# Modulation products brought forward by one stage in a two-layer diffusion backbone

## The chip, the cores and the metric

The kernel runs on one core of a Trainium2 chip. The metric is the device time of one execution in microseconds (us). PE is TensorE (PEld its weight loads), DVE VectorE, ACT ScalarE, POOL GpSimd, SP SyncE, whose queue issues most DMAs. A PSUM bank holds 128x512 floats; the kernel has eight.

## The reference: what is computed

Two layers work on 256 latent tokens of width 1024 beside 256 context tokens. Each layer first makes six modulation vectors of width 1024 for the latent and six for the context stream: `silu(c) @ w_mod[l] + b_mod[l]`. Vectors 0 and 1 (shift and scale) modulate the normalised input of the input projection. Vector 2 is the gate of the attention's result, 3 and 4 modulate the input of the mixture of experts, and 5 is its gate. Then come the input projection, three kinds of attention with 16 heads in all, an output projection with a residual and a layer norm, a router that picks two of 32 experts for a token, and the experts, with a second residual and norm. Only the latent stream is returned, so the second layer leaves the context tokens out after its attention.

## The kernel before, in words

One large function writes the whole program out. A scheduler then puts the instructions of each engine in a fixed order: an instruction that comes earlier in the program goes first, unless its inputs or its buffer are not there yet by the scheduler's own reckoning, in which case a later one may be put ahead.

**Weights** arrive as tiles of up to 1 MB (128 partitions of 2048 floats) in the order of one list, `stream`. `pump` (lines 146 to 164) issues loads from the head of the list while the tiles that are loaded and unused fill at most `cap[0]` units of 1 MB and a unit is free; it is called after each tile that is dropped. SP issues the loads, except those of experts whose number the router decides: these go through POOL (line 142) and can only be issued when the routing is done. The cap is 6 units at the start, `AC[0]` = 5 from the first layer's input projection on, `OC[0]` = 3 in its output projection and `MC[0]` = 11 ahead of its experts.

**Modulation** comes in three groups of two vectors for each layer, 8 tiles of 1 MB to a group. `mod_steps(l, g)` (lines 310 to 330) makes 8 steps for group 1 or 2: a step takes one tile and multiplies it by the activated conditioning, four products of 128 x 512 into the four column groups of one bank of tag "e" (line 320). The last step adds the bias and turns the result over with four transposes in `mod_cols` (line 369). `mod0_steps(l, tag)` (lines 332 to 362) does group 0 in another layout. Here a step has two halves: `one(j)` multiplies one tile (eight products of 128 x 256, line 347) and ACT copies the result out of its bank (line 351); `two(j)` turns that copy over with two transposes into a second bank (line 357), and DVE reduces it and adds the bias (lines 358 and 360). For the second layer the banks are of tag "a", of which there are four.

These steps are the **fillers**: functions in a list, which `fill(n)` takes from the front and runs at the place where it is called. For the first layer's run the list holds 24 steps: group 1 and group 2 of layer 0, then group 0 of layer 1. The first layer's own group 0 is no filler; it is made inside `lead` (lines 541 to 567), with the first columns of the input projection.

**The first layer's stages**, in order: `lead`, the rest of the input projection (`p_b`, `p_cq`, `p_qa`, `p_v`, lines 742 to 748; every product there is done as three passes over split operands, lines 455 to 457, after `split` has made the two parts on ACT and DVE, lines 449 and 450), a short stage that builds heads (lines 795 to 824), the attention, the output projection with the router, and the experts. The attention is a loop over 24 units and two empty rounds: each round issues `score(u)`, which takes two banks of tag "a" for the scores (lines 872 and 874) and hands them to DVE (line 882) and ACT (line 884) for the softmax, then `turn(u - 2)` (transposes, lines 896 and 902, and after every third unit the product with the values, lines 917 and 923), then one filler. In layer 0 a filler is taken only while more than 8 are left, so 16 are used in the attention and 8 remain.

The output projection runs over four blocks of 128 tokens with a lag of two blocks: `stage1(b)` does the products and the norm (`deepnorm`, whose last instruction is ACT at line 436), `stage2(b)` transposes the result (line 1054), modulates it (lines 1059 and 1061) and computes the router's logits (lines 1064 to 1066), `stage3(b)` transposes back (line 1073). `route` follows after every second block. The 8 steps that remain are taken there: `FA` gives 3 after `stage1(3)`, `FI` gives 2 and 4 after `stage2(2)` and `stage2(3)`. After it DVE finishes the routing (up to line 1403), PE gathers the tokens for the first experts (line 1189), and `up` (line 1202) starts the experts. The experts' results are computed in 14 passes; their weights, 96 tiles, follow the list's earlier tiles.

Of the kernel before, what the change touches and what calls it, by code (L numbers as in the profile page):

```python
# [31 lines left out]
MC = (11, 15)  # L32
HRD = (4, 4)
HRE = 8
FI = (0, 0, 2, 4)
LAG = 2
FA = (0, 0, 0, 3)
AC = (5, 8)
HOME = 2
HC = (8, 7, 4, 5)  # L40
# [77 lines left out]
def backbone(ctx: ExitStack, tc, ins, out):  # L118
# [11 lines left out]
    def scratch():  # L130
        return sm.tile([128, 512], F32, name="scr", bufs=5)
# [41 lines left out]
    def add(key, ap, n):  # L173
        stream.append((key, ap, n))
# [3 lines left out]
    def stream_mod(l, g, a=0, b=8):  # L178
        for j in range(a, b):
            src = ins["w_mod0"][l, j] if g == 0 else ins["w_mod"][l, (g - 1) * 8 + j]  # L180
            add(("mod", l, g, j), src, UNIT)

    def stream_chunk(k, l, c):
        add((k, l, c), ins["w_in_" + k][l, c], 4 * CH[k])

    def stream_b(l, c):
        add(("inb", l, c), ins["w_in_b"][l, :, c * 1024:c * 1024 + 1024], 1024)

    def stream_out(l):
        for c in range(4):  # L190
            add(("out", l, c), ins["w_out"][l, c], UNIT)
# [34 lines left out]
    add(("sm", 0), ins["w_small"][0], 1888)  # L226
    for c in range(2):
        stream_b(0, c)
    for c in range(2):
        stream_chunk("cq", 0, c)  # L230
    for c in range(2, 4):
        stream_b(0, c)
    for c in range(2):
        stream_chunk("qa", 0, c)
    stream_b(0, 4)
    for c in range(2):
        stream_chunk("v", 0, c)
    stream_mod(0, 1)
    stream_mod(0, 2)
    stream_out(0)  # L240
    stream_mod(1, 0)
    stream_exp(0)
    for k in ("qa", "cq"):
        for c in range(2):
# [131 lines left out]
    fillers = []  # L376

    def fill(n=1):
        for _ in range(n):
            if fillers:  # L380
                fillers.pop(0)()
# [77 lines left out]
    def layer(l, first, before=None, after=None, rest_of=None):  # L459
        nb = 4 if l == 0 else 2  # L460
# [51 lines left out]
        def defer(f):  # L512
            later.append([3, f])
# [140 lines left out]
        def p_cq():  # L654

            for b, p in chunk("cq", lat):
                bs = slice(b * 128, (b + 1) * 128)
                w = scratch()
                c_rms(p[:, 0:256], 256, w[:, 0:256])

                def turn(w=w, bs=bs):
                    pc = bank("c")
                    for i in range(2):
                        PE.transpose(pc[:, i * 128:(i + 1) * 128], w[:, i * 128:(i + 1) * 128], ident)
                    for i in range(2):
                        S.activation(CQT[:, i, bs], pc[:, i * 128:(i + 1) * 128], AF.Copy, scale=cg[:, i:i + 1])

                defer(turn)

        def p_qa():  # L670

            for b, p in chunk("qa", lat):
                qa = a_heads(p[:, 0:384], 6, 0, b)

                def turn(qa=qa, b=b):
                    pc = bank("c")
                    for i in range(3):
                        PE.transpose(pc[:, i * 128:(i + 1) * 128], qa[:, i * 128:(i + 1) * 128], ident)
                    S.activation(QKA[:, 0:3, b * 128:(b + 1) * 128], pc[:, 0:384].rearrange("p (c t) -> p c t", c=3),
                                 AF.Copy)  # L680

                defer(turn)

        def p_b(c):

            if c == 0:
                for k, K, n in ((qb, QB, nq), (kb, KB, 512)):
                    k.extend(mem.get(n) for _ in range(3))
                    K.extend(x.v(n) for x in k)
            w = split(take(("inb", l, c)), 1024)  # L690
            drop(("inb", l, c))
            pump()
            n = 256 if (last and c < 2) else 512
            wv = [x.v(8, 128) for x in w]
            p = bank("a")
            for j in range(8):
                three(p[:, 0:n], [x[:, j, :] for x in wv], hpart(j, slice(0, n)), j == 0, j == 7)
            if c < 2:
                S.activation(QB[c][:, 0:n], p[:, 0:n], AF.Copy, scale=0.125)
            elif c < 4:  # L700
                S.activation(KB[c - 2], p, AF.Copy)
            else:
                S.activation(QB[2][0:64, :], p[0:64, 0:nq], AF.Copy, scale=0.125)
                V.tensor_copy(KB[2][0:64, :], p[64:128, :])
            for x in w:
                x.free()
            tick()
# [20 lines left out]
        if l == 0:  # L728
            for b in range(4):
                xn[b] = mem.get(D)  # L730
                if b % 2 == 0:
                    load_x(b // 2)
                ln(X[b], xn[b].v(D))
            pump()

            gains()
            p_kc(lead("kc"))
            for b in range(4):
                xn[b].free()
            pump(AC[0])  # L740
            for c in range(2):
                p_b(c)
            p_cq()
            for c in range(2, 4):
                p_b(c)
            p_qa()
            p_b(4)
            p_v()
        else:
            gains()  # L750

            with tc.high_priority(4000):
                together(*[before(b, xn) for b in range(2)])
            rest_of()
            for c in range(2):
                presplit("qa", c)
            make_h()
            fill(4)
            for j in range(0, 8, 2):
                turned([(j, 0), (j + 1, 0)])  # L760
            for b in range(2):
                xn[b].free()
            together(*[before(b, xn) for b in range(2, 4)])
            p_qa()
            p_cq()
            for c in range(2):
                p_b(c)
            for j in range(0, 8, 2):
                turned([(j, 1), (j + 1, 1)])
            for b in range(2, 4):  # L770
                xn[b].free()
                xb[b].free()
            after()
            p_kc(chunk("kc", every))
            for c in range(2, 5):
                p_b(c)
            p_v()
            pump(AC[1])
# [149 lines left out]
        for u in range(len(units) + 2):  # L928
            if u < len(units):
                score(u)  # L930
            if u >= 2:
                turn(u - 2)
            if l or len(fillers) > 8:
                fill(1)
        for k in [qka] + qb + kb + vv + bia + pb + ptl + ptc + kc + qch:
            k.free()
        pump()
# [141 lines left out]
        for b in range(nb + lag):  # L1079
            if b < nb:  # L1080
                stage1(b)
                if nb == 4:
                    fill(FA[b])
            if b >= lag:
                c = b - lag
                stage2(c)
                if c < nb - 1:
                    stage3(c)
                if nb == 4:
                    fill(FI[c])  # L1090
                if c % 2:
                    route(c - 1)
        stage3(nb - 1)
# [599 lines left out]
```

## Time and profile before

| | |
|---|---|
| three timed runs | 1101.15, 1103.41, 1105.05 us; median 1103.41 us |
| the profiled execution's own time | 1108.46 us |
| its span, first to last instruction | 1106.6 us |
| busy share of the span | PE 90%, PEld 52%, DVE 46%, ACT 32%, POOL 28% |
| mean granted TensorE clock | 0.961 of full speed |
| DMA | 300.54 MB, 272 GB/s over the span |

A busy share is a mean over stages with different limits. The ends of matmuls are modelled, so a PE that counts as busy is not always at its peak, and a few matmul records are missing. Starts are recorded: the cost of a step on PE is best read as the distance from its start to the start of the next one. In the profile's fp32 rows each matmul of the program stands as two instructions, so x8 is four products.

### The profile page before, as it was taken

Reading aid. Unit: us, or ns where it says so; the run is one execution under the profiler, and the core shown is the slowest. Engines: PE = TensorE matmul, PEld = TensorE weight load, DVE = VectorE, ACT = ScalarE, POOL = GpSimd, SP = SyncE. Lnnn points to the kernel's source line nnn. Section 1 sums busy time; section 2 is a strip of 40 time slices with the busy share of each in tenths; the row PEclk is TensorE's granted clock in tenths of the full one; section 3 lists DMA queues with packets and bytes.
Section 4 is the critical chain, followed back from the end, with each engine's and each line's share of the span. In section 5 each row is a group of like instructions: output and inputs, shape, how many; then the busy total and the mean of one; then the engine's idle time right before and its main releaser. Section 6 shows DMA issues by size and latency. Waiting matters only on the chain. (4 is left out here: it accounts for less than half of the span.)

```text
span 1106.6 us, 14809 instructions
## 1 busy us (share of the span) xinstructions
PE 998.9 (90%) x5525; PEld 577.0 (52%) x5525; DVE 512.7 (46%) x1364; ACT 349.3 (32%) x708; POOL 305.2 (28%) x325
## 2 busy tenths in 40 slices
PE   4899999999999999999983789999997899999894
PEld 2689744466866454444430378844466554433231
DVE  4653457775567211100016687267655654242244
ACT  3543155572442011111111385144544222111111
POOL 2021143340000433243333132042300045334420
PEclk9999999999999999999996889999987899999997
DMA  9813147601169999999999653446325799999992
GB/s 372 321 37 115 48 181 275 230 27 51 76 267 374 398 400 423 351 412 422 423 422 414 235 183 119 172 162 216 127 78 232 302 378 421 421 422 420 422 420 94
DMA packets 46208, 300.54 MB, mean 272 GB/s; under 512 B 5395, under 2 KB 5779, under 8 KB 14389
## 3 DMA queue, kind: packets, MB, share of 16 engines
q0 software_dynamic: 25824, 177.81, 39.2%
q1 hardware_dynamic: 20308, 121.75, 29.3%
q8 instruction: 45, 0.74, 0.3%
q14 instruction: 31, 0.25, 0.1%
HBM read 292.19 MB, written 7.34 MB: 271 GB/s over the span
## 5 line engine op out<-in xcount | busy, mean ns | idle before, releaser
L142 POOL DMA_INDIRECT u<-in_w_exp,u x162 | 162.5, 1003 | 305.5 <-PE psa L1202 100.1
L1202 PE MATMUL psa<-u,u 128*32 128x512 f32 (+2 forms) x1040 | 218.1, 602 | 23.8 <-DMA u<-in_w_exp,u 23.7
L1202 PEld LDWEIGHTS psa<-u,u 128*32 128x32 f32 (+2 forms) x1040 | 65.5, 127 | 152.7 <-issue 110.6
L455 PE MATMUL psa<-u,u 128*128 128x512 f32 (+3 forms) x400 | 142.8, 360 | 0.9 <-ACT u L504 0.7
L456 PE MATMUL psa<-u,u 128*128 128x512 f32 (+3 forms) x400 | 141.7, 355 | 2.0 <-DVE u L450 2.0
L457 PE MATMUL psa<-u,u 128*128 128x512 f32 (+3 forms) x400 | 140.3, 354 | 0.1
L1189 PEld LDWEIGHTS psc<-u,u 128*128 128x128 f32 x640 | 83.6, 198 | 33.2 <-issue 30.1
L1189 PE MATMUL psc<-u,u 128*128 128x256 f32 x640 | 94.3, 298 | 3.0 <-DVE u L1175 2.1
L887 POOL TENSOR_SCALAR u<-u,ri 128x512 f32<-128x512 f32 (+1 forms) x48 | 68.5, 1431 | 99.2 <-DVE ri L885 81.7
L1209 DVE TENSOR_TENSOR scr<-scr,psa 128x256 f32<-128x256 f32 x26 | 10.9, 421 | 168.5 <-ACT scr L1208 168.5
L456 PEld LDWEIGHTS psa<-u,u 128*128 128x128 f32 x400 | 77.3, 193 | 12.9 <-DVE u L450 4.2
L455 PEld LDWEIGHTS psa<-u,u 128*128 128x128 f32 x400 | 77.1, 193 | 11.5 <-ACT u L504 1.1
L457 PEld LDWEIGHTS psa<-u,u 128*128 128x128 f32 x400 | 76.5, 192 | 9.8 <-issue 1.2
L884 ACT ACTIVATE u<-psa,nm 128x512 f32<-128x512 f32 (+1 forms) x96 | 58.4, 615 | 55.0 <-DVE nm L882 50.1
L1260 PE MATMUL pse<-u,scr 128*64 128x512 f32 (+1 forms) x288 | 67.4, 599 | 0.6 <-DMA u<-in_w_exp,u 0.6
L1208 ACT ACTIVATE scr<-psa 128x256 f32<-128x256 f32 x26 | 10.0, 385 | 175.8 <-PE psa L1202 175.8
L450 DVE TENSOR_TENSOR u<-u,u 128x1024 fp32r<-128x1024 f32 (+4 forms) x38 | 56.2, 1485 | 19.5 <-ACT u L449 19.4
L1191 ACT ACTIVATE u<-psc 128x512 f32<-128x512 f32 x52 | 31.1, 597 | 101.9 <-PE psc L1189 59.6
L882 DVE TENSOR_REDUCE nm<-psa 128x1 f32<-128x512 f32 (+1 forms) x80 | 53.2, 683 | 13.1 <-PE psa L872 9.5
L1247 PE MATMUL pse<-u,scr 128*32 128x512 f32 (+2 forms) x232 | 57.3, 600 | 1.4 <-ACT scr L1237 1.4
L419 POOL TENSOR_TENSOR lns<-lns,mhalf 128x1 f32<-128x1 f32 x22 | 15.3, 699 | 156.4 <-DVE lns L418 126.2
L449 ACT ACTIVATE u<-u 128x1024 fp32r<-128x1024 f32 (+4 forms) x38 | 47.5, 1266 | 14.2 <-PE psa L456 4.6
(317 smaller groups left out, 1361.6 us busy)
## 6 DMA issues: line engine op xcount, KB each, us to landing
u<-in_w_mod SPq DMA_DIRECT2D x48, 1024.0 KB, 6.0
u<-in_w_exp SPq DMA_DIRECT2D x30, 1024.0 KB, 7.2
u<-in_w_out SPq DMA_DIRECT2D x8, 1024.0 KB, 4.8
ys<-u SPq DMA_DIRECT2D x12, 512.0 KB, 8.1
u<-in_w_in_b SPq DMA_DIRECT2D x10, 512.0 KB, 11.8
u<-in_w_in_v SPq DMA_DIRECT2D x4, 960.0 KB, 4.6
u<-in_w_in_qa SPq DMA_DIRECT2D x4, 768.0 KB, 11.4
u<-in_ln_rows SPq DMA_DIRECT2D x6, 512.0 KB, 7.1
```

Source lines behind the costliest of these rows:

```text
L142: G.indirect_dma_start(out=b.ap(UNIT), out_offset=None, in_=wexp_rows, in_offset=bass.IndirectOffsetOnAxis(ap=idx, axis=0), bounds_check=N ...
L450: V.tensor_tensor(l_[:, c], w[:, c], h[:, c].bitcast(F32), OP.subtract)
L455: PE.matmul(p, lhsT=a[0], rhs=b[0], start=first, stop=False)
L456: PE.matmul(p, lhsT=a[0], rhs=b[1], start=False, stop=False)
L457: PE.matmul(p, lhsT=a[1], rhs=b[0], start=False, stop=final)
L882: V.tensor_reduce(out=nm[:, s, 0:n], in_=pv, axis=AX.X, op=OP.max, negate=True)
L884: S.activation(P[:, i, :], pv[:, i, :], AF.Exp, bias=nm[:, s, i:i + 1], accum_out=su[:, s, i:i + 1])
L887: (G if s == 0 else V).tensor_scalar(P[:, i, :], P[:, i, :], ri[:, s, i:i + 1], None, op0=OP.mult)
L1189: PE.matmul(pv[:, j, :], lhsT=H[b][:, k * 128:(k + 1) * 128], rhs=OH[:, b, :], start=(b == 0 and i == 0), stop=(b == nb - 1 and i == 1))
L1202: PE.matmul(g[r, :], lhsT=XG[:, k, at * 128 + r.start:at * 128 + r.stop], rhs=W(t, k // 4).v(4, 512)[:, k % 4, :], start=(k == 0), stop=(k ...
L1247: PE.matmul(y[r, :], lhsT=hc[:, c * 128 + r.start:c * 128 + r.stop], rhs=W(t, 2).v(2, D)[:, c, f * 512:f * 512 + 512], start=(c == 0), sto ...
L1260: PE.matmul(y[r, :], lhsT=hc[:, c * 128 + r.start:c * 128 + r.stop], rhs=W(t, 2).v(2, D)[:, c, f * 512:f * 512 + 512], start=(c == 0), sto ...
```

## The change

The eight steps of layer 0's group 1 are taken within the first layer's input projection: one after each of the first four `p_b`, two after `p_cq` and two after `p_qa`. Their tiles are put into the list between the weights of these parts. In the attention every round takes a filler, without a condition: these are now layer 0's group 2 and layer 1's group 0, 16 steps in 26 rounds. The list has layer 1's group 0 ahead of the output projection's weights instead of behind them. The output projection takes no fillers, and `FI` and `FA` are gone.

```diff
-FI = (0, 0, 2, 4)
-FA = (0, 0, 0, 3)
...
     for c in range(2):
         stream_b(0, c)
+        stream_mod(0, 1, c, c + 1)
     for c in range(2):
         stream_chunk("cq", 0, c)
+    stream_mod(0, 1, 2, 4)
     for c in range(2, 4):
         stream_b(0, c)
+        stream_mod(0, 1, c + 2, c + 3)
     for c in range(2):
         stream_chunk("qa", 0, c)
+    stream_mod(0, 1, 6, 8)
     stream_b(0, 4)
     for c in range(2):
         stream_chunk("v", 0, c)
-    stream_mod(0, 1)
     stream_mod(0, 2)
+    stream_mod(1, 0)
     stream_out(0)
-    stream_mod(1, 0)
     stream_exp(0)
...
             for c in range(2):
                 p_b(c)
+                fill()
             p_cq()
+            fill(2)
             for c in range(2, 4):
                 p_b(c)
+                fill()
             p_qa()
+            fill(2)
             p_b(4)
             p_v()
...
-            if l or len(fillers) > 8:
-                fill(1)
+            fill()
...
             if b < nb:
                 stage1(b)
-                if nb == 4:
-                    fill(FA[b])
             if b >= lag:
                 c = b - lag
                 stage2(c)
                 if c < nb - 1:
                     stage3(c)
-                if nb == 4:
-                    fill(FI[c])
                 if c % 2:
                     route(c - 1)
```

## Rows read from the trace of the kernel before

**Rows 1.** Windows: us, busy of PE, PEld, DVE, ACT, POOL, clock, DMA share, GB/s.

```profile
0.00:50.60 50.60, 32.77 (x272) 22.41 (x272) 27.11 (x109) 22.66 (x36) 8.00 (x30) 0.97 0.90 360
50.60:139.80 89.20, 85.98 (x453) 74.05 (x454) 38.03 (x99) 27.73 (x61) 17.24 (x22) 1.00 0.22 73
...
147.40:257.20 109.80, 106.72 (x668) 56.03 (x666) 78.92 (x176) 63.24 (x168) 44.83 (x35) 0.98 0.53 190
...
306.90:345.80 38.90, 34.81 (x319) 25.84 (x318) 31.15 (x153) 16.46 (x38) 1.10 (x2) 0.96 0.74 302
345.80:612.00 266.20, 236.40 (x1211) 106.75 (x1210) 49.19 (x128) 40.32 (x73) 93.04 (x92) 0.96 0.98 401
```

**Rows 2.** Timeline of PE, experts' first product and last wait: start, us, line, idle before.

```profile
345.82 7.09 PE L1202 MATMUL psa<-u,u 128*64 128x512 f32 x32
...
601.87 1.97 PE L1202 MATMUL psa<-u,u 128*64 128x512 f32 x2 [15.87 <-DMA u<-in_w_exp,u]
```

**Rows 3.** Timeline of SP's queue and of POOL: loads ahead of the experts.

```profile
297.77 7.97 SPq L161 DMA_DIRECT2D u<-in_w_mod  x6
305.79 30.15 SPq L161 DMA_DIRECT2D u<-in_w_exp  x10
...
353.19 1.20 POOL L142 DMA_INDIRECT u<-in_w_exp,u  x1 [36.96 <-DVE find L1403]
```

**Rows 4.** Windows around the start of the experts, columns as in rows 1.

```profile
322.00:332.00 10.00, 10.00 (x107) 6.67 (x110) 7.03 (x46) 4.43 (x12) 0.00 (x0) 1.00 0.02 9
332.00:353.00 21.00, 18.82 (x126) 12.87 (x126) 20.48 (x104) 3.78 (x10) 0.00 (x0) 0.92 0.96 381
353.00:365.00 12.00, 12.00 (x72) 6.72 (x74) 1.11 (x2) 3.84 (x6) 4.27 (x5) 1.00 0.92 349
365.00:440.00 75.00, 72.55 (x438) 36.77 (x433) 10.55 (x38) 9.86 (x19) 29.65 (x30) 1.00 1.01 411
```

**Rows 5.** Timeline of PE in the first layer's attention: a filler step and its turn.

```profile
181.49 0.66 PE L369 MATMUL psc<-ident,u 128*128 128x128 f32 x4
...
183.73 1.07 PE L320 MATMUL pse<-u,csil 128*32 128x512 f32 x8
184.72 1.13 PE L872 MATMUL psa<-u,u 64*128 64x512 f32 x4
```

**Rows 6.** Waits of PE from 50 to 138 us, the longest: total, times, longest.

```profile
PE psa L456 <- DVE u L450: 1.6, 1, 1.6
```

**Rows 7.** Timeline of PE in the output projection's end: two halves of a group 0 step.

```profile
313.57 0.44 PE L357 MATMUL psa<-ident,scr 128*128 128x128 f32 x2
313.93 1.07 PE L347 MATMUL psa<-u,csil 128*32 128x256 f32 x16
314.94 0.87 PE L1054 MATMUL psc<-ident,u 128*128 128x128 f32 x6
```

**Rows 8.** Timeline of PE and ACT: scores of two units, last read of the first's banks.

```profile
196.84 1.13 PE L872 MATMUL psa<-u,u 64*128 64x512 f32 x4
...
199.92 1.13 PE L872 MATMUL psa<-u,u 64*128 64x512 f32 x4
...
202.02 0.19 ACT L884 ACTIVATION_READ_ACCUMULATOR u<-psa,nm 128x1 f32 x1
```

**Rows 9.** Timeline of PE, ACT and DVE from `stage1(3)` to the last logits.

```profile
306.65 0.39 PE L457 MATMUL psa<-u,u 128*128 128x512 f32 x1
...
316.01 1.87 PE L1064 MATMUL psa<-u,u 128*128 128x36 f32 x16
...
316.51 1.24 ACT L436 ACTIVATE u<-u,lns 128x1024 f32<-128x1024 f32 x1 [0.43 <-DVE modT L358]
...
324.94 1.51 ACT L1061 ACTIVATE u<-psc,modT,modT 128x128 f32<-128x128 f32 x4 [0.17 <-PE psc L1054]
...
329.97 0.16 DVE L1065 TENSOR_TENSOR lg<-psa,tabl 128x4 f32<-128x4 f32 x1 [2.06 <-PE psa L1064]
```

**Rows 10.** Timeline of PE: its first product.

```profile
12.75 0.69 PE L487 MATMUL psc<-ident,u 128*128 128x128 f32 x2 [12.75 <-ACT u L409]
```

## The prediction

> **What bounds the kernel now.** I first cut the span at the borders of its stages and looked at each stage's windows [rows 1]. In the first layer's input projection PE is busy for 85.98 of 89.20 us, in its attention for 106.72 of 109.80 us, both at a granted clock of 0.98 or more: there PE sets the pace, and DMA is far from full (shares 0.22 and 0.53). The end of the output projection, 306.9 to 345.8 us, is another kind of stage: PE is busy for 34.81 of 38.90 us, but DVE for 31.15 as well, and a chain of small steps over ACT, DVE, POOL and PE leads through norm, logits and routing. The experts, 345.8 to 612 us, are where DMA is full (0.98), and near the end PE stands 15.87 us for weights [rows 2].
>
> So the question is which of two clocks the experts go by. Their weights come in 96 tiles, ten of them issued from 305.8 us on, before the routing is known [rows 3]; then the units are full. The next ones that need the router come at 353.19 us, and what POOL waited for is DVE's last routing instruction. Between 322 and 332 us DMA is almost still (9 GB/s), from 332 to 353 it loads what fits (381 GB/s), from 353 to 365 it drops to 349, and only then is it full, at 411 [rows 4]. The queue of weights has thus run empty when the routing ends. From there on the whole stage hangs on that instant, and the time of the kernel moves with it, one for one. I therefore count what the change does to the arrival of the routing, through PE's work and PE's waits ahead of it.
>
> **The change, part by part.** No product is added or taken out: eight group 1 steps move from the attention to the input projection, eight group 0 steps of layer 1 from the end of the output projection to the attention. The count comes out: 8 and 16 are all 24.
>
> *Input projection.* One step holds PE from 183.73 to 184.72, 0.99 us, with the change of shapes before and after it included; the turn that closes the group takes 0.66 us [rows 5]. Eight steps and a turn are 8.6 us. On the other side, PE stands for 3.2 us in this stage (89.20 - 85.98) [rows 1], the longest for 1.6 us on DVE's half of a split [rows 6]. A step that is ready can stand in such a wait. I take 2.0 us as absorbed: **+6.6 us**, ends +5.4 (all absorbed) and +8.6 (none). The 8 MB of tiles cost nothing in themselves: 8.4 MB at 411 GB/s is 20 us of a queue whose share here is 0.22. They do go through SP's queue ahead of the b, cq, qa and v weights, and the cap of five units leaves these two to three parts of lead, where all of them used to be far ahead. If a tile were late, its split, then PE, would wait; a load is 2.55 us by that rate and the stage's eight parts last 11 us each in the mean, so I count nothing, and put it into the upper end of the range. The group's bias load and memset go to POOL in a stage in which POOL is busy for 17 of 89 us: nothing. The last step's add and copy move from a DVE at 72% (78.92 of 109.80) to one at 43%: nothing.
>
> *Attention.* It loses those 8.6 us and gets eight steps of group 0. `one` holds PE from 313.93 to 314.94 (1.01 us) and `two` from 313.57 to 313.93 (0.36) [rows 7]: 8 x 1.37 = 11.0 us, so **+2.4 us** of work. There is a new wait as well. `two` needs ACT's copy of `one`, which stands in ACT's queue behind the softmax, and both halves need banks of tag "a", of which the scores use two a unit. A unit's scores begin at 196.84, the next ones at 199.92, and the first one's banks are only read out at 202.21 [rows 8]: at 199.92 all four are taken. With a step in between, the next scores may be held for up to 202.21 - 199.92 = 2.3 us, of which the step's own 1.37 us are counted already; 0.9 us a unit, eight units, is 7.3 us at most. At least it is nothing, since `turn(u - 2)` can go ahead in the meantime and every third round has the long product with the values. The trace has no such case in an attention; between 0 and 7.3 I take **+3 us**, a little under the middle for the work that can go ahead. What is held behind a waiting step in PE's queue is the next unit's scores, and DVE's maximum and ACT's exponentials wait for those. The output's weights keep their place after 16 modulation tiles; nothing changes for them.
>
> *End of the output projection.* It loses the 11.0 us of group 0. That is not what it gives back. The last block's products end at 307 us, and its norm on DVE, ACT and POOL ends with ACT at 316.51 + 1.24 = 317.75, whatever PE does [rows 9]. After that come its transposes (eight, 1.1 us by [rows 7]), the modulation (1.51 us) and the logits (1.87 us): 322.3 us at the earliest. Now the logits land at 329.97. So **at most 7.7 us** come back, and the rest of the 11.0 turns into PE standing idle. Two blocks are ahead in the queue, with 1.1 + 1.87 + 1.1 us each and two waits for the modulation: 8.2 + 3.0 us fit between 307 and 318 only just. I take 1 us off: **-6.7 us**; the other end is half of the 7.7, -3.9, if the three blocks get in each other's way on ACT and DVE.
>
> The sum is 6.6 + 2.4 + 3 - 6.7 = **+5.3 us**, with ends +0.1 (5.4 + 2.4 + 0 - 7.7) and +14.4 (8.6 + 2.4 + 7.3 - 3.9). The profiled execution took 1108.46 us in all, so its like after the change takes 1113.8. That execution was 5.05 us above the median of the runs, 1103.41; on the median the forecast is 1108.7 us. Two things push the ends outward. The granted clock falls when PE has waits close together: 0.92 over the 21 us from 332 to 353 [rows 4], which is some 1.7 us, and an emptier output projection may pay that once more. And `lead` has PE busy for 32.77 of 50.60 us [rows 1]; early steps may slip into its waits.
>
> The profile's stages can be read with a rule of the Trainium skill, page Perfetto Trace Analysis, section Optimization Strategy: where the most-contended engine changes over time, interleaving the regimes may help. It speaks against this change, which takes filling work out of a latency chain and puts it where PE is the limit. By the rule alone the products were free at the end of the output projection and give nothing back: the sum would be +12.0. The rows bear it out in part, PE being busy there for 34.81 of 38.90 us with them in place.
>
> **The rivals.** *The tail returns nothing.* The chain through norm and routing sets the arrival of the logits by itself, and the change pays 6.6 + 2.4 + 3 = 12.0 us: 1115.4. (It is the time that the rule of the Trainium skill named above would give.) For it: DVE is busy for 31.15 of 38.90 us there. Against: three blocks' work on PE stands behind the fillers in its queue. The jam of the score banks at its full 7.3 us comes to nearly the same time, +9.6.
>
> *It cancels.* The waits of the input projection swallow all of their 3.2 us, the scores are never held, and the tail gives 7.7: +0.1 us, 1103.5. For it: the scheduler can put other ready work ahead of a held step. Against: all three ends have to fall together, or two of them and half of the third.
>
> *The weights gain.* This one ends on the other side. Eight tiles of modulation leave the stretch right ahead of the experts (six are issued from 297.77 on [rows 3]), 20 us of DMA. If more expert weights are then in place when the routing ends, PE's 15.87 us at the end shrink, up to all of them: 5.3 - 15.9, so 1092.8 us. It decides at 5.3 us: from there on the gain outweighs the cost. Against it: the units are full in both kernels when the routing ends, by the cap, and the queue has run empty by then [rows 4]; earlier loads only wait longer. For it: 21 us at 381 GB/s from 332 us on are 8 MB, so most of the ten tiles were still to load then.
>
> *The scheduler lifts early steps into `lead`.* PE stands there for 17.8 us, 12.75 of them before its first product [rows 1, 10]. Filling the other 5 us takes the input term to 8.6 - 3.2 - 5 = +0.4, and with the best ends of the other two it is -4.9 us: 1098.5. Against: DMA is at 0.90 there, with the tiles of group 1 last in line.
>
> **How the numbers follow.** A measurement can tell this kernel from no change at about 0.3%, 3.3 us. The forecast, +3.3 to +9, has 0.38. The tail that returns nothing, or the full jam, 0.12: slower in all 0.50. Cancelling has 0.27, which is the share for no change. The weights' gain has 0.13 and the lifted steps 0.10: faster 0.23. The range goes from 1098 (the lifted steps) to 1119 (the upper end, 1117.8, with the clock's 1.7 us rounded); it leaves out most of the weights' gain and little else.
>
> **What would show it.** In the profile after, the input projection should last 5 to 8 us longer with PE at its busy share; the attention should show group 0 products (line 347) and some waits of scores on ACT or of line 357 on line 351; from the last block's products to the last logits it should take 15 to 18 us instead of 23, with PE idle in between; line 1202 should start about 5 us later, and the first load of POOL by as much. The prediction is wrong if POOL's first load comes earlier than 353 us, or if the stage from there to the end of layer 0's experts gets shorter than it is.

## The result, and the profile after

The change made the kernel slower: 1120.35 us (median of 4 runs, 1118.62 to 1121.99) against 1102.28 us of the kernel before beside it (4 runs). The ratio is 1.0163, 95% interval 1.0140 to 1.0186: 18.1 us. The forecast, 1108.7, had the sign and less than a third of the size; the range ended 1.35 us short. The times are of fast runs; one slow run of a kernel further below, of 1293.06 us, is left out.

The profiled execution of after took 1120.03 us, its span 1118.2. The first profile of before, on which the prediction rests, took 1108.46, 6 us over its median, so stages are compared with a second one (first experiment below; time 1099.5, span 1097.6). Windows of that second profile, columns as in [rows 1]: from the first product of the `b` part to the first scores; attention, to the first product of `mod_bcast`; products of the output projection; from the last block's product to the first expert product (line 1202), called the end below; experts, to the end of their last long wait.

```profile
48.70:145.49 96.79, 93.65 (x479) 77.93 (x479) 41.39 (x105) 30.92 (x67) 18.31 (x23) 1.00 0.21 70
145.49:253.53 108.04, 104.98 (x665) 55.13 (x665) 78.86 (x176) 63.08 (x168) 44.75 (x35) 1.00 0.53 193
253.53:303.37 49.84, 49.32 (x233) 39.12 (x236) 27.46 (x56) 18.01 (x26) 3.33 (x6) 1.00 0.17 64
303.37:341.98 38.61, 34.52 (x319) 25.60 (x319) 30.89 (x152) 16.45 (x38) 1.10 (x2) 0.96 0.75 302
341.98:595.29 253.31, 227.29 (x1196) 104.73 (x1195) 47.48 (x128) 40.08 (x72) 92.76 (x92) 0.97 1.00 409
```

The same windows of the kernel after:

```profile
49.94:158.78 108.84, 104.32 (x546) 80.92 (x545) 44.02 (x106) 30.81 (x65) 17.16 (x23) 0.98 0.36 128
158.78:272.97 114.19, 108.22 (x741) 57.99 (x740) 81.83 (x190) 66.05 (x176) 45.36 (x35) 1.00 0.51 183
272.97:322.81 49.84, 49.32 (x231) 39.34 (x231) 27.48 (x56) 18.00 (x26) 3.33 (x6) 1.00 0.00 1
322.81:360.46 37.65, 30.80 (x174) 28.39 (x173) 30.75 (x140) 13.99 (x30) 1.10 (x2) 0.64 0.60 228
360.46:613.19 252.73, 226.97 (x1196) 104.17 (x1195) 46.66 (x124) 40.07 (x72) 92.69 (x92) 0.98 0.98 402
```

Row by row the second column gives +12.05, +6.15, 0.00, -0.96 and -0.58 us. The first three stages and the end make +17.24, which is about the 18.1 of the medians. What else differs between these two executions, 1.24 us ahead of the first window and 2.70 behind the last, is of the size by which two profiles of the same kernel differ. In the fourth row of after lies the surprise: PE has less to do than before (30.80 against 34.52 us), takes nearly as long, and its granted clock is 0.64.

The rows of after that answer to [rows 2, 3], from the timelines of PE and of POOL:

```profile
360.46 4.08 PE L1202 MATMUL psa<-u,u 128*64 128x512 f32 x18
...
613.19 1.11 PE L1202 MATMUL psa<-u,u 128*64 128x512 f32 x1 [15.88 <-DMA u<-in_w_exp,u]
```

```profile
367.83 1.20 POOL L140 DMA_INDIRECT u<-in_w_exp,u  x1 [36.37 <-PE psa L1202]
```

PE's first expert product, POOL's first load and the 15.9 us wait at the end all come later together, by 18.5, 18.5 and 17.9 us against the second profile of before. The kernel's time does hang on the arrival of the routing.

### The profile page after: what moved, and what is told of

Read it like the earlier page. It is cut to its first block, busy times and chain, and to the rows that moved or that the text cites. A ratio compares the mean times of both kernels' runs of the same rounds, so it can differ in the third digit from the quotient of the medians.

```text
span 1118.2 us, 14808 instructions
## 1 busy us (share of the span) xinstructions
PE 1007.6 (90%) x5525; PEld 585.5 (52%) x5525; DVE 516.4 (46%) x1364; ACT 349.0 (31%) x708; POOL 302.8 (27%) x325
```

## The experiments

**The kernel before, again** (unchanged).

> The kernel before, unchanged, for a second profile: the first one's execution took 1108.46 us, 6 us above the median of the runs (1102.28). If a stage of it was disturbed, this profile shows which: input projection 96.8, attention 109.7, from the last block's product to the first expert product 39.2, experts to their last long wait 256 us in the first one. All theories expect about 1102 here, and the stages that they compare are taken from this profile if it is nearer to the median.

It took 1099.5 us. It is the second profile above. Against the first one it starts its `b` part 1.9 us earlier, its attention is 1.7 us shorter (108.04 against 109.73 by the same window) and its experts 2.7 us (253.31 against 256.05). The 3.3 us by which after's experts seemed shorter are this spread: 252.73 against 253.31.

**The two parts of the change alone**, each as a difference from the kernel after. First only the input projection:

```diff
-HC = (8, 7, 4, 5)
+HC = (8, 7, 3, 5)
...
-    stream_mod(1, 0)
     stream_out(0)
+    stream_mod(1, 0)
...
-            fill()
+            if l or len(fillers) > 8:
+                fill(1)
...
+                if nb == 4:
+                    fill(FA[b])
...
+                if nb == 4:
+                    fill(FI[c])
```

> Only the first part of the change: group 1 in the input projection, everything else as before (eight steps of group 2 in the attention, layer 1's group 0 in the end of the output projection; one cap of layer 1's loads at the end of the experts is 3 instead of 4 for want of room). If the parts add up: input projection 108 (as after), attention 109.7 less eight steps of 0.99 to 1.07 us = 101 to 102, end of the output projection 39.2 (as before), time 1102.3 + 11.3 - 8.3 = about 1105. Of the experts' stage, 256.1 us before and 252.7 after from the first product to the last long wait: 256 if the loads of layer 1's group 0 ahead of the experts cost them those 3.3 us (as before, they stand right ahead of them here), 252.7 if it is something of the input part.

1106.41 us (10 runs) against 1101.81, ratio 1.0045 (1.0028 to 1.0062). `HC` caps loads at the end of the first layer's experts, behind the stages that are compared below. Then only the attention, with the input projection as before:

```diff
-        stream_mod(0, 1, c, c + 1)
...
+    stream_mod(0, 1)
     stream_mod(0, 2)
     stream_mod(1, 0)
...
             for c in range(2):
                 p_b(c)
-                fill()
...
```

> Only the second part of the change: group 1 stays in the attention (24 steps there: groups 1 and 2 and layer 1's group 0), nothing in the input projection, nothing in the end of the output projection. If the parts add up: input projection 96.8 (as before), attention 108.0 in the second profile of before plus eight steps of 1.37 us = 119, up to 124 with the waits of the score banks, end of the output projection 37.6 (as after), so the time is 1101.8 + 11 to 16 - 1 = 1112 to 1117. If the change were more than its parts (the end of the output projection costs only in company with the later start), 1108 or less.

1112.55 us against 1101.98, ratio 1.0097 (1.0072 to 1.0123). Windows of the first of the two, input projection and attention:

```profile
50.86:159.44 108.58, 104.05 (x546) 80.69 (x545) 44.01 (x106) 30.81 (x65) 17.16 (x23) 0.98 0.36 128
159.44:262.44 103.00, 99.14 (x597) 53.90 (x596) 76.74 (x174) 63.48 (x168) 44.51 (x35) 0.98 0.34 121
```

and of the second, attention and end:

```profile
146.80:266.13 119.33, 115.78 (x809) 60.20 (x808) 82.80 (x192) 66.25 (x176) 42.93 (x35) 1.00 0.66 236
...
315.96:353.30 37.34, 30.49 (x176) 28.08 (x173) 30.41 (x139) 14.00 (x30) 1.10 (x2) 0.63 0.61 229
```

By stages the parts add up, and the ratios of the times come near it (1.0045 and 1.0097 against 1.0163). The input projection pays 11.8 us; for taking its eight steps away the attention gives back 5.0 (108.04 - 103.00; from the second kernel to after it is 119.33 - 114.19 = 5.1). Group 0 costs the attention 11.3 and gives back 1.3 at the end. Where the 3.4 us between 8.5 and 5.1 went is seen by taking busy from length: PE stands 3.55 us in the attention with 24 steps and 5.97 in that of after, with 16. The steps there had been filling waits, so 7.56 us of busy time went and 2.42 us of waiting came. Of this, 1.72 us are a wait for POOL in the last rounds, which the kernel with 24 steps does not have: its last step ends at 260.8 us of 266.1, that of after at 233.1 of 273.0. The timeline of PE in after:

```profile
267.67 0.33 PE L907 MATMUL psc<-ident,u 128*128 128x128 f32 x1 [1.12 <-POOL u L892]
268.60 0.55 PE L907 MATMUL psc<-ident,u 128*128 128x128 f32 x3 [0.60 <-POOL u L892]
```

In the first kernel waiting rose by 0.80 us only, from 3.06 to 3.86; but behind the same wait for POOL its clock fell (0.98 in its row; more on this in the last section).

**The turn that closes group 1.** Of the 12.05 us of the input projection, 10.67 are busy time (8.7 the eight steps, by their group; 1.1 the closing turn; the rest slower products) and 1.38 more waiting: one wait of 3.39 came, others of 2.0 went. The timeline of PE in after:

```profile
113.54 0.39 PE L456 MATMUL psa<-u,u 128*128 128x512 f32 x1
117.32 1.11 PE L370 MATMUL psc<-ident,u 128*128 128x128 f32 x4 [3.39 <-DVE u L326]
...
118.66 0.63 PE L458 MATMUL psa<-u,u 128*128 128x512 f32 x1
...
121.01 0.39 PE L458 MATMUL psa<-u,u 128*128 128x512 f32 x1
```

and of DVE:

```profile
114.47 0.56 DVE L602 TENSOR_TENSOR scr<-psa,ars 128x384 f32<-128x384 f32 x1 [1.22 <-POOL ars L399]
...
116.57 0.69 DVE L326 TENSOR_TENSOR u<-pse,u 128x512 f32<-128x512 f32 x1
```

The turn (line 370) stands at the head of PE's queue and waits 3.39 us for the bias addition (line 326), which DVE reaches only behind the norms of the `qa` heads, themselves waiting for POOL. Behind it a product takes 0.63 us where it takes 0.39 at full clock. Two runs move the closing. The first makes it the attention's first filler, the second puts it ahead of `qa`:

```diff
+                def close():
...
+                if (l, g) == (0, 1):
+                    fillers.insert(0, close)
+                else:
+                    close()
```

> The kernel after, with the closing of the first layer's group 1 (bias, turn and copy) as the first filler of the attention instead of the input projection. Theory of the turn: the 3.4 us wait of the turn behind DVE's split, and the slower clock behind it (0.87 and 0.96 in two windows of 10 us, 1.7 us in all), leave the input projection: from the first product of its b part to the first scores it takes 103 to 105 us instead of 108.8, and the time is 4 to 5 us shorter, 1115 to 1117. Rival, late weights or the SP queue make the excess: 107.5 to 109 us as before, less only the turn's 0.7 to 1.1 us, time 1119 to 1121.

```diff
...
             for c in range(2, 4):
                 p_b(c)
-                fill()
+                fill(2)
             p_qa()
-            fill(2)
```

> The kernel after, with group 1 closed one part earlier (two steps after each of the third and fourth part of b, none after qa; the loads in the same order). In the run that closed it later the input projection was 3.6 us shorter and the attention 3.8 longer. Theory of the turn's place: a closing that has no split in front of it on DVE waits for nothing, and nothing of it moves to the attention: input projection 105 to 106.5 instead of 108.8, time 1116.5 to 1118.5. Rival, wherever it closes, DVE's split is then late for the next products and the wait comes back: 108 to 110, 1119 to 1122.

Later: 1120.63 us (median of three runs), ratio 1.0171 (1.0140 to 1.0203). Earlier: 1116.62 us, 1.0143 (1.0114 to 1.0172). Both expectations name DVE's split; by the rows it is the head norms that stand in front. Windows of the second run:

```profile
50.46:156.18 105.72, 102.38 (x545) 79.74 (x545) 44.47 (x106) 31.08 (x65) 17.20 (x23) 1.00 0.36 131
156.18:273.50 117.32, 111.33 (x742) 58.92 (x741) 81.97 (x190) 66.18 (x176) 45.36 (x35) 0.97 0.50 178
```

The input projection is 3.1 us shorter, as the theory wanted (3.6 in the first run: 105.27). But its attention is 3.1 us longer, with the same instructions and the same waiting (117.32 - 111.33 = 5.99 against 5.97): the clock is 0.97 there. It fell to 0.50 behind a wait of 1.12 us for ACT and behind the one for POOL, both of which after has too, at 1.00. The time of the second run is 3.7 us under after, of the first 0.3 over; their intervals overlap with after's, so that the closing costs after some 3 us is shown for the stage, not for the time.

**The banks of the scores.** The prediction feared a jam at banks "a".

```diff
-    one, two = mod0_steps(1, "a")
+    one, two = mod0_steps(1, "e")
```

> The kernel after, with the banks of layer 1's group 0 taken from the two of the values (tag e) instead of the four of the scores (tag a). Theory of the jam: the scores no longer share their banks with the steps, and the attention's 6.1 us over the second profile of before (114.2 against 108.0) shrink to the 2.4 to 3.5 us of work alone: time 3 us shorter, 1116 to 1118. Rival, the excess is the chain of ACT's copies in the queue of the softmax and PE's own work, whatever bank they use: 114 or more, time 1119 to 1123 (longer if the values now wait for a bank).

1120.23 us, as after. In after no score waits for a bank. What is new there against before stands in the stretch with the steps of group 0, 2.86 us in two pairs like this one:

```profile
211.98 0.55 PE L901 MATMUL psc<-ident,u 128*128 128x128 f32 x3 [1.11 <-ACT u L913]
...
216.19 0.44 PE L358 MATMUL psa<-ident,scr 128*128 128x128 f32 x2 [0.32 <-ACT scr L352]
```

The first is a transpose of `turn`, held until ACT has copied out an earlier one; the second is the step's own transpose, held by ACT's copy of `one`. The attention with banks "e":

```profile
157.64:272.23 114.59, 111.02 (x741) 59.37 (x740) 80.47 (x190) 65.82 (x176) 44.46 (x35) 0.99 0.51 182
```

PE waits 3.57 us here instead of 5.97; the two long waits for ACT are gone, in an order in which PE takes the scores ahead of these transposes. But it is busy 2.80 us longer, in part because the clock fell behind POOL in this execution (the last section has 1.7 us for such a fall). So the scores do not jam; whether other banks would save the 1 us or so that this fall may hide stays open.

**The end, with PE kept busy.** Windows of two us of after, behind the last block's product (322.81):

```profile
324.00:326.00 2.00, 2.00 (x16) 1.77 (x15) 2.00 (x7) 1.50 (x4) 0.00 (x0) 1.00 0.80 332
326.00:328.00 2.00, 0.45 (x3) 0.30 (x2) 1.59 (x4) 1.01 (x3) 0.55 (x1) 1.00 0.98 414
328.00:330.00 2.00, 0.77 (x4) 0.77 (x5) 1.99 (x8) 0.67 (x1) 0.00 (x0) 0.74 1.04 438
330.00:332.00 2.00, 1.62 (x8) 1.22 (x6) 1.48 (x8) 1.51 (x4) 0.55 (x1) 0.50 0.79 332
...
354.00:356.00 2.00, 2.00 (x11) 2.00 (x11) 1.97 (x6) 0.60 (x1) 0.00 (x0) 0.50 0.00 0
356.00:358.00 2.00, 2.00 (x18) 2.00 (x18) 2.00 (x10) 0.60 (x1) 0.00 (x0) 0.94 0.00 0
```

PE is busy for 0.45 and 0.77 of two us, and the granted clock goes to its lower level (0.50, 1.2 GHz) for 26 us. The Trainium skill, page TensorE: Matmul & The Clock Gate, section A second HAM failure mode: psum-queue depth-cycling, tells of a kernel in which short idle spells of PE between groups of products make the clock swing between its levels; these rows agree in that the clock falls behind such spells, but it falls once and stays down.

The other profiles agree. In the six whose kernels have the eight steps in this place the end's clock is 0.96 (38.57 to 38.79 us), in the five whose kernels have nothing in their place it is 0.63 or 0.64 (37.34 to 37.65 us).

Five runs add products into a bank that nobody reads. In the first they stand where the steps of group 0 stood (64 products), in the second around the logits (56; the expectation counts 64), in the third between them (36):

```diff
+        def warm(n):
+            p = bank("e")[:, 0:256]
+            for _ in range(n):
+                for k in range(8):
+                    i = k % 4
+                    PE.matmul(p[32 * i:32 * i + 32, :], lhsT=csil[:, k, :], rhs=tab[:, 0:256], ...
...
                 stage1(b)
+                if nb == 4 and b == 3:
+                    warm(3)
...
```

> The kernel after, with eight groups of eight products in the end of the output projection where the modulation steps stood, into a bank that nobody reads; no load, no copy and no turn is added. Theory of the clock: PE, left without the steps, stands in short waits there and its granted clock falls to 0.50 for 26 us, so that its own transposes, logits and gathers take twice as long. Then the clock stays near 1.0, the stretch from the last block's product to the first expert product shrinks from 38.0 to 31 to 35 us, and the time falls by 3 to 7 us, to 1113 to 1117, although PE is given more to do. Rival, the chain over DVE, ACT and POOL sets this stretch whatever PE's clock is: 38 us or more as before, time 1119 to 1123.

> The kernel after, with 64 products into an unread bank in the end of the output projection as in the first such run, but 24 of them now lie in the stretch in which PE waited in the kernel after (326 to 330 us, between the last block's products and its next logits), and the rest around the last two blocks' logits. In the first such run the clock fell all the same (0.50 from 334 to 342 us) and the last logits came 2.2 us later than after. Theory of the clock: with the waits filled it stays at 1.0 up to the last logits, which come 16 to 20 us after the last block's product instead of 22.1, and the first expert product 32 to 36 us after it instead of 37.65; time 1115 to 1119. Rival, the chain over DVE and ACT sets the logits whatever the clock: 22 us or more, 38 us or more, 1120 to 1123.

> The kernel after, with 36 products into an unread bank laid between the logits of the second and third block of the first layer (24 and 12), where PE waited in the kernel after, and none behind them. Earlier 64 such products made the end of the output projection 2.7 us shorter in the profile (34.9 against 37.65), but 40 of them stood ahead of the last block's work. Theory of the clock: with fewer, the clock stays at 1.0 until the third block's logits, and the last logits come 17 to 20 us after the last block's product (22.1 after), the first expert product 32.5 to 35.5 us (37.65); time 2 to 5 us under after, 1115 to 1118. Rival, the chain over DVE and ACT: 37 us or more, 1119 to 1121.

1119.27, 1119.05 (1114.70 to 1123.09) and 1120.92 us; none can be told from after. The ends took 37.22, 34.93 and 37.55 us. The first and the third settle little: in the first the products stood ahead of the second block's transposes, the clock fell from 334 us on all the same, and the last logits came 24.3 us after the last product; in the third they held up a logit. In the second the clock was mostly held, and the end is 2.7 us shorter than in after:

```profile
322.69:357.62 34.93, 30.71 (x285) 23.39 (x282) 28.88 (x129) 13.55 (x30) 1.10 (x2) 0.95 0.66 246
```

In two more runs each added product reads the modulated block between whose logits it stands:

```diff
             for j in range(8):
                 PE.matmul(p[:, 0:36], lhsT=HR[:, j, :], rhs=wr[:, j, :], ...
+                if nb == 4 and b and j in (1, 3, 5):
+                    warm(HR, j, (0, 8, 3, 0)[b])
```

> The kernel after, with 33 products into an unread bank, each reading the modulated block whose logits it stands between (24 in the second block's, 9 in the third's), so that none can stand ahead of that block's modulation; in the run before, products of the third block had slipped ahead of the second block's last logit and held it 3 us. Theory of the clock: it stays at 1.0 to the third block's logits, and part of the half-speed work behind (transposes, logits and gathers, some 15 us at 0.50) runs at 1.0: the first expert product comes 33 to 36 us after the last block's product instead of 37.65. Rival, the chain: in the second layer's end of the output projection the clock was held at 1.0 by such products from 833 to 869 us and the stretch lasted 27.3 us against 27.9 to 28.7; if that holds here, 37 to 38.

> As warm_tied, with 12 products in the third block's logits, 6 in the last block's and 16 behind them, ahead of the routing's products and the gathers. Theory of the clock: 1.0 nearly throughout, first expert product 31.5 to 35 us after the last block's product; time 3 us or more under after, if the executions' own spread of some 4 us lets it show. Rival, the chain over DVE: 36.5 us or more although the clock is 1.0.

1118.58 (1114.99 to 1124.58) and 1122.77 us (1118.86 to 1123.59), again not to be told from after by their intervals (1.0125 to 1.0207 and 1.0145 to 1.0212); the profiles tell more. Windows of the first, the end and two short ones:

```profile
323.02:357.71 34.69, 28.24 (x240) 22.59 (x238) 30.14 (x137) 13.85 (x30) 1.10 (x2) 0.95 0.65 247
332.00:334.00 2.00, 1.65 (x14) 1.09 (x14) 1.90 (x12) 2.00 (x4) 0.52 (x1) 1.00 0.05 20
```

and of the second:

```profile
322.07:363.50 41.43, 38.63 (x290) 27.84 (x288) 28.77 (x129) 13.79 (x30) 1.10 (x2) 0.75 0.56 207
332.00:334.00 2.00, 2.00 (x14) 1.00 (x13) 1.40 (x7) 1.53 (x3) 0.00 (x0) 0.50 0.02 8
```

With 33 products more than after, the end is 3.0 us shorter at a clock of 0.95, and the last logits come 20.0 us after the last product instead of 22.1. The second kernel has the same instructions up to 332 us and the same two waits ahead of them (0.80 and 0.58 us). This time the clock fell there, and what was added behind ran at half speed. So by these profiles the clock costs after some 3 us at the end; the times of the runs, which spread by more than that, do not show it. It is not the whole of what was missing, as a timeline of the first kernel shows, ACT, DVE and PE in turn:

```profile
332.87 1.26 ACT L437 ACTIVATE u<-u,lns 128x1024 f32<-128x1024 f32 x1
```

```profile
338.33 1.29 DVE L1089 TENSOR_TENSOR u<-psc,u 128x512 fp32r<-128x512 f32 x2
```

```profile
339.17 1.16 PE L1065 MATMUL psc<-ident,u 128*128 128x128 f32 x8 [0.81 <-DVE u L1089]
```

The last block's norm is ready at 334.1, 11.1 us after its last product. Its transposes start at 339.17: they want a bank of tag "c", and both still hold the third block, until DVE has subtracted its halves (line 1089 of that kernel, in `stage3`), which comes behind the third block's logits, its transposes back and ACT's copies of them. In after it is 338.81, 16.0 us after the last product against 16.15 here. The point is as late at the higher clock, but here nine of the added products (1.7 us) stand between the third block's logits; how much earlier it would come without them was not run. From there to the first expert product after takes 21.65 us, this kernel 18.54: that is where the clock counts.

**Both repairs together**, the earlier closing and the third form of the added products.

> The kernel after with two of the changes that were tried on it, the earlier closing of group 1 and the 36 products between the logits. If the two losses are independent, their gains add: 3.7 us of the closing (measured alone) and 2 to 5 of the clock, 1111.5 to 1114.5. If both act on the same thing (the time goes wherever PE waits next), 1116 or more.

1116.26 us, ratio 1.0147 (1.0102 to 1.0193): as the closing alone. They don't add, since in that form the products saved little (end 36.90).

**The same on the kernel before.** In the end of the second layer PE waits 2.2, 2.7 and 3.7 us; 98 products were added into these waits. And the last unit's scaling was moved from POOL, for which PE waits 1.7 us, to ACT:

```diff
+                    if s == 0 and u == len(units) - 1:
+                        S.activation(P[:, i, :], P[:, i, :], AF.Copy, scale=ri[:, s, i:i + 1])
+                    else:
```

> The kernel before, with 98 products into an unread bank in the end of the second layer's output projection, where PE waits 2.2, 2.7 and 3.7 us and its granted clock is 0.50 from 839 to 858 us in the second profile: 28 behind the last block's products, 30 between the logits, 40 ahead of the routing's products. No load, copy or other work is added. Theory of the clock: it stays at 1.0, the transposes, logits and gathers there (about 12 us of PE at half speed) take half, and what of it is on the path, 3 to 6 us, is saved: 1096 to 1099 against 1102. Rival, DVE's chain sets this stretch whatever PE's clock is, or the added products delay it: 1101 to 1104.

> The kernel before, with one multiplication moved: in each layer's attention the last unit's scores of the first head are scaled by ACT instead of POOL. PE waits 1.1 and 0.6 us for POOL there at the end of the first layer's attention, with the same instructions in all kernels, and behind that wait the granted clock fell to 0.50 for some 4 us in three profiles (the first one of before, the one with the input part alone, the two closings) and stayed at 1.0 in others. Theory of the clock: without the wait both go, 1.0 to 1.7 us for the wait and up to 1.7 us where the clock fell, in the first layer, and half of it in the second: 1.5 to 4 us faster than before, 1098 to 1100.5. Rival, ACT's queue is as late as POOL (exponentials and copies stand in front), or DVE's splits are next: within 1 us of before.

1100.53 us (12 runs) against 1103.05 (23), ratio 0.9985 (0.9966 to 1.0003), and 1100.90, 0.9987 (0.9968 to 1.0007). Windows from the second layer's last output product to its first expert product, first in the second profile of before:

```profile
832.81:860.66 27.85, 18.11 (x103) 16.51 (x100) 20.69 (x89) 11.21 (x22) 1.10 (x2) 0.63 0.78 312
```

then with the products:

```profile
833.16:860.44 27.28, 26.28 (x297) 17.79 (x298) 18.87 (x77) 11.12 (x22) 1.10 (x2) 1.00 0.74 297
```

The clock is held at 1.00 throughout, and 0.6 us come of it. Two effects stand behind the 0.6, as the gathers ahead of the first expert product show, first in the second profile of before, then with the products:

```profile
854.81 5.92 PE L1189 MATMUL psc<-u,u 128*128 128x256 f32 x32 [1.05 <-DVE u L1175]
```

```profile
856.44 4.07 PE L1202 MATMUL psc<-u,u 128*128 128x256 f32 x32 [1.00 <-DVE u L1089]
```

From their start to the first expert product it is 4.00 us instead of 5.85. But they start 23.28 us after the last output product instead of 22.00: the last 40 of the added products stand ahead of the second block's transposes back, for whose result (line 1089) the gathers wait. So the second half of the rival holds, the products delay the stretch; that DVE's chain alone sets it is not shown.

The moved scaling shortens the attention by 2.48 us (105.56) and lengthens the next stage by 1.35 (51.19), which makes 1.13 over both. The 1.35 are no wait: PE is busy for 51.08 of the 51.19 us, and the last products with the values (1.0 us) now stand behind the border of the two stages. In place of POOL PE waits 0.8 us for ACT and 0.2 for DVE at the attention's end.

> The kernel before with both of the changes tried on it: the last unit's scaling on ACT in both layers, and the products that hold the clock in the end of the second layer's output projection. Each alone was 2.2 and 2.5 us under before, neither beyond its interval. If they add, 4 to 5 us faster, 1098 to 1099 against 1102 to 1103; if they are noise, within 1.5 us.

1100.21 us (12 runs) against 1102.66, 0.9988 (0.9970 to 1.0005). They don't add, and none of the three beats the kernel before beyond its interval.

## Why the prediction was wrong, step by step

**Input projection, predicted +6.6, measured +12.05.** The absorption of 2.0 us came: without the wait of the turn PE waits 1.1 us here instead of 3.14, and the 1.6 us wait of [rows 6] is gone. The work was sized too low: 8.6 us by [rows 5], 9.8 measured (8.7 the steps, 1.1 the turn) and 0.9 of slower products. The larger part is one wait: the turn that closes the group stands for 3.4 us. "The last step's add and copy move from a DVE at 72% to one at 43%: nothing" is the step that failed. A share of a stage does not say what stands in front of one addition; the row at that place does, and there the head norms stand in front. The lower clock behind the wait is seen in the turn and the products after it. Late weights and SP's queue, counted at nothing, were nothing: none of PE's waits in the stage is for a DMA.

**Attention, predicted +5.4, measured +6.15.** By the two rows PE is busy 3.24 us longer (+2.4 predicted) and waits 2.91 us longer (+3). The sum is right, the reason for its second term only in part. Line 358 (357 before) does wait for ACT's copy, 0.64 us in all; the scores, which were to be held by the banks, are not held, and 2.2 us are transposes that wait for ACT. That the "+3" fits is partly luck. Group 0 alone came at +11.3, close to the 11.0 of [rows 7]. The prediction asked whether a step that comes in can hide in a wait and did not ask whether a step that goes out had covered one: from 24 steps to 16, the eight gave back 5.1 us instead of the 8.5 that they hold PE for, since 2.4 us of waits came out from under them.

**End, predicted -6.7, measured -0.96.** This is the larger failure, 5.7 us. The chain through the norm was right: 10.7 us after the last product predicted, 11.1 seen. The step "8.2 + 3.0 us fit between 307 and 318 only just; I take 1 us off" failed: the third block leaves the banks only 16 us after the last product (17.2 in both profiles of before; the prediction read the end of the norm there and not the start of the transposes). So the last logits came 22.1 us after the last product instead of the 15 to 18 that the prediction named as its sign. With the clock mostly held the end is 34.69 us (with the 33 products), 3.9 less than before, so up to 2.8 of the missing 5.7 are this chain. The other 3 are the clock, which the text had put at 1.7 us in the range's upper end and at nothing in the sum. The work taken out of the waits is what had kept the clock up: 0.96 in all six profiles with it and 0.63 or 0.64 in all five without. Added products replace it only at times (0.75 to 0.95).

**What moved one for one.** The experts' stage kept its length (252.73 against 253.31), and the gain from earlier weights did not come. The cap holds them, as the prediction argued.

**The rivals.** "The tail returns nothing" was nearest: the end gave back 1.0 of 11.0 us of work. By the Trainium skill, page Perfetto Trace Analysis, section Optimization Strategy, whose rule speaks for interleaving stages with different limits, this was the case to expect, as the prediction applied the rule; the runs agree with it. It had a chance of 0.12 with the full jam, too little. Even its 1115.4 lacked the 5.4 us by which the input projection was put too low.

## What to carry to other kernels

Work that lies in a latency chain's gaps costs little there and its full time elsewhere. Price it where it goes by its distance from start to start, and where it leaves by the waits and the granted clock that appear without it. Products added to hold the clock are work too: they help only where nothing that the stretch waits for stands behind them. Before counting a small operation on another engine as hidden, read the row of that engine at the very place where the next instruction will wait for it.

## What the runs showed of the hardware that was not expected

The granted clock does not follow from the instructions and waits alone. At the end of the attention PE waits 1.1 and 0.6 us for POOL in fourteen of the seventeen profiles; the others are the two with the moved scaling and the one with 24 steps. Behind these waits the clock fell to its lower level in six of the fourteen and stayed at 1.00 in eight. In the second profile of before it kept its clock:

```profile
247.53:249.53 2.00, 0.71 (x4) 0.45 (x4) 1.26 (x3) 0.27 (x1) 1.57 (x2) 1.00 0.61 135
249.53:251.53 2.00, 2.00 (x16) 1.13 (x16) 1.79 (x2) 0.57 (x1) 0.00 (x0) 1.00 0.99 418
```

and in the first it did not:

```profile
251.17:253.17 2.00, 2.00 (x9) 1.20 (x9) 1.42 (x2) 0.00 (x0) 0.00 (x0) 0.77 0.90 377
253.17:255.17 2.00, 2.00 (x11) 1.15 (x12) 1.47 (x1) 0.60 (x1) 0.00 (x0) 0.50 0.17 70
```

That is the 1.7 us between the two attentions (109.73 and 108.04). Falls of this kind come and go between executions, and runs of one kernel spread over up to 10 us (1096.37 to 1106.36 for before, 23 runs). What decides at such a wait whether the clock falls stays open here. And what the lower clock costs hangs on what else a stretch waits for: 26 us of it cost some 3 us in the first layer's end, some 19 us of it between 0.6 and 1.9 us in the second's.
